# A two-layer encoder: the first MLP's down projection as seven products, and the conditioning in other pieces and on another engine

## The chip, the cores and the metric

The kernel runs on one core of a Trainium2 chip. A core has TensorE (PE in the profile; its weight loads are PEld) for matrix products, VectorE (DVE), ScalarE (ACT) and GpSimd (POOL) for elementwise work, and SyncE (SP), which here issues nearly all DMA transfers. The metric is the device time of one execution in microseconds (us), as the median of several runs.

## The reference

One inference step of two layers over 1024 prompt tokens and 32 sample tokens, of width 1024, with an MLP of hidden width 4096. The prompt and the sample each have one conditioning vector c. For layer l:

```python
u   = x * (1 + sc1) + sh1                       # sh, sc, g: six parts of silu(c) @ w_ada[l] + b_ada[l]
y   = mlstm(u)                 (layer 0)  or  band_attention(u)  (layer 1)
x   = layer_norm(ALPHA * x + (1 + g1) * y, ln_g[l, 0], ln_b[l, 0])
u   = x * (1 + sc2) + sh2
f   = jnp.square(jax.nn.relu(u @ w_up[l])) @ w_down[l]
x   = layer_norm(ALPHA * x + (1 + g2) * f, ln_g[l, 1], ln_b[l, 1])
```

Layer 0 mixes with an mLSTM (four heads, causal convolution, gated matrix memory in chunks), layer 1 with attention over a band of chunks and a shared key and value projection, which has a conditioning of its own (`w_ada_kv`). The outputs are the two final x, and the caches and states of the mixers. All is fp32.

## The kernel before

**Tokens and precision.** All T = 1056 tokens lie in the free dimension, the features on the 128 partitions, 8 rows deep. There are two ways to cut the tokens: blocks `TBS` of 384, 384 and 288, and quarters of `QN` = 264. An fp32 product is done in three matmuls: each operand is split into a high part (rounded by ScalarE) and the rest (subtracted by VectorE, `split`), and `proj` (L110 to L120) adds high by high (L118), high by low (L119) and low by high (L120) into one PSUM bank. There are eight banks.

**Layout in SBUF.** `U` holds the modulated input u, high and low, for all tokens; `uap` is a view of it. `acc` holds x, and takes the gated outputs; in the first layer it is three tiles, one for each block. A ring has three `raw` rooms (weights as they are loaded) and six `wc` rooms (their split forms). `wblock` loads 512 rows by 256 columns of a weight into a raw room and splits it. `tmp_t` gives one of five small rooms.

**Order.** The program is written as a stream of matmul groups. Beside it `Flow` keeps a list of side tasks, written as generators; every group of matmuls calls `flow.tick(columns / 96)`, and a task that has yielded a number goes on when so many ticks have passed; `flow.finish` runs a task to its end at once. A quarter's tile of an up projection is 2.75 ticks. The order of each engine's instructions follows this text, except where a region gives PE's order by hand (the seven products, L1314 on). A DMA on SP's queue waits there for the room it fills, and the DMAs behind it wait too.

**Stages.** PE runs through: the first projections; the mLSTM; its output projection (`out_proj`, L988), whose last step for a block starts a side task `norm` that also writes u for the MLP into U; the first MLP (`mlp`, L1006); q, keys and values; the attention; its output projection; the second MLP (`mlp7`, L1118); the last norm, which goes out by rows.

**The first MLP, `mlp`.** The hidden width goes in eight groups of 512. For each group there are four up tiles by three token blocks (`up`, L1016), kept in five `h` rooms as high and low of the squared relu, and eight down tiles by three blocks (`down`, L1031), each of which VectorE adds into acc with the gate (`add_gated_at`). Up of the next group is interleaved with down of this one. In the last group the ups are ordered so that the first block's down, and with it the norm that q needs, comes before the last ups (L1075 to L1080).

**The second MLP, `mlp7`.** Up goes first and whole: 16 pieces of 256 hidden features, by quarters (`up_tile`, L1166). Two hidden halves by two token halves make a 2x2 block, and down is a 2x2 by 2x2 block product in Winograd's form with seven products in place of eight. ScalarE and VectorE make seven operand forms of each piece (tiles `H`, three rooms, and `HL`, one room), and SP stores them to DRAM (`hd`, 1848 KB a piece and token half). The first 14 of the 16 pieces go this way, in four groups `GRP` of 3, 4, 3 and 4; the last two are done plainly: up in `up_plain` (L1180), stored to `hpl`, and down in the usual three matmuls at the end. Before the products, `forms` (L1221) makes the seven weight forms of a pair of output tiles from four blocks of w_down, and `Rooms` (L1103) hands out SBUF rooms into which `fill` loads operands `fx` by SP; some rooms are free at once (`f4`), others are what held u, free when the up has read it (`L.rooms`). `prep(i)` starts the loads of unit i's weights, the following steps of its generator do the sums and the splits. Up goes on `up_weights` loaded during the attention's output projection (`early_up`), so that PE finds weights there. `L1` holds what differs by layer.

**The conditioning.** `ada_cols` (L225) computes silu(c) @ w_ada without PE: for each 256 columns, the 1024 weight rows come in two loads of 512; VectorE multiplies each of the 8 rows of 128 by a scalar per partition and adds up (`aacc`, L238 and L241), once for the prompt and once for the sample, then transposes and reduces; PE sums what is left over partitions in four small matmuls per 1024 columns. Layer 0's part runs as a side task in the mLSTM (`ada_l0`, in one room of the ring, `ada_room`); the first 2048 columns of it come earlier. All of layer 1's and the key/value part (`ada_rest`, L1382) runs as a side task of the first MLP, from the third block's first up on, with waits `ADA_B` of 4, 2 and 1 ticks. It ends with `combine`, which folds a norm's gain and the conditioning together, and with `bias_table` for the attention; the first MLP's last norm waits for it (L1400).

## Time and profile before

| | |
|---|---|
| median of three runs | 2478.76 us (2478.34 to 2480.81) |
| profiled execution, its own time | 2479.81 us |
| its span | 2478.0 us, at a mean granted clock of 0.992 |
| PE, share of the span | 97% |
| DVE, ACT, POOL | 71%, 41%, 7% |
| DMA | 318.10 MB, 128 GB/s over the span |

A line of the groups reads: line of the kernel, engine, operation, output <- inputs by the program's names, partitions x elements, count, then busy time of the group and mean ns of one, then the idle time of the engine just before them with what ended most of it. A line that starts with a time is one instruction (or a run of equal ones): start, duration in us, engine, line, operation. For PE the durations of single matmuls overlap, so the steps between starts tell its pace. "granted clock" is TensorE's clock as the throttle let it run, as a share of full speed.

### The profile page before, as it was taken

The page shows a single profiled execution, that of the slowest core. Times are in us where ns is not written, and L with a number is a line of the kernel's source. Part 1 is how long each engine was busy: PE and PEld are TensorE (multiplying, and loading weights), DVE is VectorE, ACT ScalarE, POOL GpSimd, SP SyncE. Part 2 cuts the span into 40 slices and gives each one's busy share as a digit, 9 for nine tenths or more (in the row PEclk, how much of TensorE's full clock was granted, in tenths as well). Part 3 has the DMA queues.
Part 4 walks back from the last instruction along what each step waited for, and adds up shares of the span by engine and source line. Part 5 has one row for each costly group of instructions (what it writes and reads, how often), then busy time and mean ns, then how long its engine had stood idle before and what let it go on. Part 6 is the DMA issues. An engine that isn't in the chain of part 4 may idle for free.

```text
span 2478.0 us, 42688 instructions
## 1 busy us (share of the span) xinstructions
PE 2413.7 (97%) x16844; PEld 2315.4 (93%) x16844; DVE 1759.7 (71%) x4038; ACT 1016.9 (41%) x2118; POOL 168.6 (7%) x315
## 2 busy tenths in 40 slices
PE   7999999999999999999999999999999999999997
PEld 4999999999999999999999867789999999899997
DVE  4899999788679679677597667746853442776758
ACT  4644456382211212212266556654754443221212
POOL 0211100000000000000001134410000000000003
PEclk9999999999999999999999989999999999999999
DMA  8433224313224224234122310050375646767632
GB/s 297 122 110 101 84 88 129 107 35 119 77 87 137 84 86 135 80 92 142 43 98 82 91 40 1 18 147 27 134 251 212 215 179 254 262 239 273 255 130 72
DMA packets 236220, 318.10 MB, mean 128 GB/s; under 512 B 11624, under 2 KB 185084, under 8 KB 234996
## 3 DMA queue, kind: packets, MB, share of 16 engines
q1 hardware_dynamic: 236020, 315.38, 38.8%
q8 instruction: 132, 2.16, 0.4%
q14 instruction: 68, 0.56, 0.1%
HBM read 242.79 MB, written 74.91 MB: 128 GB/s over the span
## 4 chain that ended last, share of the span: by engine, by line
PE 78%; DVE 8%; DMA 6%; ACT 2%; issue 1%; POOL 0%; SPq 0%; DVEq 0%; POOLq 0%; ACTq 0%
PE up L118 10%; PE up L120 10%; PE up L119 9%; PE dn L1283 9%; PE dn L119 5%; PE dn L118 5%; PE dn L120 5%; DMA fx<-hd 3%; PE pv L1608 2%; PE pt L1588 2%; PE s L1558 2%; PE o L118 1%; PE o L119 1%; PE o L120 1%; PE op_b L118 1%
## 5 line engine op out<-in xcount | busy, mean ns | idle before, releaser
L120 PE MATMUL up<-u,w_up 128*128 128x264 f32 x1024 | 292.9, 286 | 0.0
L118 PE MATMUL up<-u,w_up 128*128 128x264 f32 x1024 | 292.4, 286 | 0.0
L119 PE MATMUL up<-u,w_up 128*128 128x264 f32 x1024 | 291.1, 284 | 0.0
L1283 PE MATMUL dn<-fx,wf 128*128 128x264 f32 x2208 | 275.3, 286 | 7.9 <-DMA fx<-hd 7.4
L1283 PEld LDWEIGHTS dn<-fx,wf 128*128 128x128 f32 x2208 | 272.2, 189 | 9.7 <-issue 4.6
L119 PE MATMUL dn<-h,w_dn 128*128 128x384 f32 (+1 forms) x768 | 249.5, 325 | 0.0
L118 PE MATMUL up<-U,w_up 128*128 128x384 f32 (+1 forms) x768 | 249.2, 324 | 0.0
L119 PE MATMUL up<-U,w_up 128*128 128x384 f32 (+1 forms) x768 | 247.9, 323 | 0.0
L118 PE MATMUL dn<-h,w_dn 128*128 128x384 f32 (+1 forms) x768 | 247.8, 323 | 0.0
L120 PE MATMUL up<-U,w_up 128*128 128x384 f32 (+1 forms) x768 | 247.6, 322 | 0.0
L120 PE MATMUL dn<-h,w_dn 128*128 128x384 f32 (+1 forms) x768 | 247.3, 322 | 0.0
L119 PEld LDWEIGHTS up<-u,w_up 128*128 128x128 f32 x1024 | 193.9, 189 | 0.0
L118 PEld LDWEIGHTS up<-u,w_up 128*128 128x128 f32 x1024 | 193.8, 189 | 0.0
L120 PEld LDWEIGHTS up<-u,w_up 128*128 128x128 f32 x1024 | 193.3, 189 | 0.0
L986 DVE SCALAR_TENSOR_TENSOR ACC<-dn,ada,ACC 128x264 f32<-128x264 f32 (+4 forms) x328 | 131.7, 426 | 86.4 <-PE dn L1283 74.6
L238 DVE SCALAR_TENSOR_TENSOR aacc<-rada,cs,aacc 128x256 f32<-128x256 f32 x448 | 190.3, 477 | 0.0
L986 DVE SCALAR_TENSOR_TENSOR acc<-dn,ada,acc 128x384 f32<-128x384 f32 (+2 forms) x256 | 119.4, 486 | 47.4 <-PE dn L120 46.3
L1025 ACT ACTIVATE r<-up 128x384 f32<-128x384 f32 (+1 forms) x96 | 44.3, 463 | 246.9 <-PE up L120 238.4
L119 PEld LDWEIGHTS dn<-h,w_dn 128*128 128x128 f32 x768 | 144.4, 188 | 0.2 <-DVE h L1028 0.2
L120 PEld LDWEIGHTS dn<-h,w_dn 128*128 128x128 f32 x768 | 144.5, 188 | 0.0
L120 PEld LDWEIGHTS up<-U,w_up 128*128 128x128 f32 x768 | 144.3, 188 | 0.0
L118 PEld LDWEIGHTS up<-U,w_up 128*128 128x128 f32 x768 | 144.2, 188 | 0.1
(354 smaller groups left out, 5957.4 us busy)
## 6 DMA issues: line engine op xcount, KB each, us to landing
hd<-HL SPq DMA_DIRECT2D x28, 1848.0 KB
raw_up<-in_w_up_dram SPq DMA_DIRECT2D x68, 512.0 KB
rada<-in_w_ada_dram SPq DMA_DIRECT2D x64, 512.0 KB
fx<-hd SPq DMA_DIRECT2D x37, 528.0 KB
raw_dn<-in_w_down_dram SPq DMA_DIRECT2D x36, 512.0 KB
ada_room<-in_w_ada_dram SPq DMA_DIRECT2D x32, 512.0 KB
fx<-hd SPq DMA_DIRECT2D x50, 264.0 KB
fx<-hd SPq DMA_DIRECT2D x16, 792.0 KB
```

The source lines that it names most:

```text
L118: nc.tensor.matmul(ps, wh, mov(0, k), start=(k == 0), stop=False)
L119: nc.tensor.matmul(ps, wh, mov(1, k), start=False, stop=False)
L120: nc.tensor.matmul(ps, wl, mov(0, k), start=False, stop=(k == nk - 1))
L238: nc.vector.scalar_tensor_tensor(acc[:, cnd], raw[:, k], sc, acc[:, cnd], op0=ALU.mult, op1=ALU.add)
L986: nc.vector.scalar_tensor_tensor(xs, ps[:, off + o:off + o + mm_], gate[:, fc, cnd:cnd + 1], xs, op0=ALU.mult, op1=ALU.add)
L1025: nc.scalar.activation(r, ps[:, :n], AF.Relu)
L1283: nc.tensor.matmul(p, ws[w][:, wl, k], t[:, s0, xl], start=first and k + n_ == 0, stop=k == kg - 1 and n_ == 2, skip_group_check=not first)
L1558: nc.tensor.matmul(s[:, b, :w], qst, kk[i][:, g, k0 + j0:k0 + j0 + w], start=(i == 0), stop=(i == 1))
L1588: nc.tensor.transpose(pt[:kp, j - j0, pr * P:(pr + 1) * P], ps_[pr][:, j * P:j * P + kp], ident)
L1608: nc.tensor.matmul(pv[64 * e:64 * e + 64, :nq], V[:kp, vt0 + j, g * 64:(g + 1) * 64], pts[e][:kp, j, :nq], start=(j == 0), stop=(j == nt - 1))
```

## The change

The first MLP also goes through `mlp7`, by a new class `L0`. `mlp` and the three-tile acc are removed; acc is one tile `ACC0`, cut into block views. Rooms for operands are U's two halves by columns, once the up has read them, so a load of rows goes to rows that lie apart. The up weights of the first pieces are loaded in the mLSTM's output projection (`early_up0`, and `up_weights(0, 0)` after the second block's end). The plain pieces' down at the end goes by the blocks `TBS`, and each block's end starts that block's norm as before. In q, ACC0's room is given up once all three norms have ended, which is asked for at the second block.

In `mlp7`, for both layers: the first unit's weight loads (`prep(0)`) are issued before the operand loads, the second unit's (`prep(1)`) before the last piece's first half; later ones (`prep(i + 2)`) one product later than before. In `forms` two of four sums are written in place. The plain pieces' results go through two rooms `hl` throughout, not partly through the ring.

The conditioning: in `ada_cols` (now used for layer 0 alone) the sample's products and sums go to GpSimd, as a multiplication into a side buffer and an addition. A new `ada_more` does the same in pieces of 512 (or 256) columns and loads of two rows of 128, each one ahead. What `ada_rest` did is cut in three: `ada_up` in the first MLP's up (columns 0 to 3071 of layer 1, the key/value part, and columns 3072 to 4095), `ada_down` in its products (4096 to 5119, in 256 columns), `ada_last` in the second MLP's up (5120 to 6143, the last gate).

```diff
                     for cnd in range(2):
                         sc = cs[:, 4 * half + k, cnd:cnd + 1]
-                        if half or k:
+                        if cnd:
+                            pr = tmp_f([P, 256], f"apr_{base}_{j}_{half}_{k}") if half or k else acc[:, 1]
+                            nc.gpsimd.tensor_scalar(pr, raw[:, k], sc, 0.0, op0=ALU.mult, op1=ALU.add)
+                            if half or k:
+                                nc.gpsimd.tensor_add(acc[:, 1], acc[:, 1], pr)
+                        elif half or k:
...
+    def ada_more(parts, nb, mk, tmp_f, raw_f, step):
+        n = nb * P
+        todo = [(src, c0, base, j, k0) for src, c0, base, nch in parts for j in range(0, nch, nb) for k0 in range(0, KC, 2)]
+        def load(i):
+            if i == len(todo):
+                return None
+            src, c0, base, j, k0 = todo[i]
+            raw = raw_f([P, 2, n], f"rada_{base}_{j}_{k0}")
+            nc.sync.dma_start(raw, src[k0 * P:(k0 + 2) * P, c0 + j * P:c0 + (j + nb) * P].rearrange(
+                "(k p) c -> p k c", p=P))
+            return raw
+        raw = load(0)
+        for i, (_, _, base, j, k0) in enumerate(todo):
+            ahead = load(i + 1)
+            yield step[0][i % len(step[0])]
+            if k0 == 0 and nb == 4:
+                accs_ = [tmp_f([P, n], f"aacc{cnd}_{base}_{j}") for cnd in range(2)]
+            elif k0 == 0:
+                acc3 = tmp_f([P, 3, n], f"aacc_{base}_{j}")
+                accs_ = [acc3[:, cnd] for cnd in range(2)]
+            for k in range(2):
+                for cnd in range(2):
+                    sc = cs[:, k0 + k, cnd:cnd + 1]
+                    if cnd:
+                        pr = accs_[1] if k0 + k == 0 else tmp_f([P, n], f"apr_{base}_{j}_{k0}_{k}") if nb == 4 else acc3[:, 2]
+                        nc.gpsimd.tensor_scalar(pr, raw[:, k], sc, 0.0, op0=ALU.mult, op1=ALU.add)
+                        if k0 + k:
+                            nc.gpsimd.tensor_add(accs_[1], accs_[1], pr)
+                    elif k0 + k:
+                        nc.vector.scalar_tensor_tensor(accs_[cnd], raw[:, k], sc, accs_[cnd], op0=ALU.mult, op1=ALU.add)
+                    else:
+                        nc.vector.tensor_scalar(accs_[cnd], raw[:, k], sc, None, op0=ALU.mult)
+            raw = ahead
+            if k0 < KC - 2:
+                continue
+            cxf = cx.rearrange("p g b -> p (g b)")
+            for cnd in range(2):
+                at = tmp_f([P, n], f"aat{cnd}_{base}_{j}")
+                nc.vector.transpose(at, accs_[cnd])
+                o0 = j % 8 * 8 + 4 * nb * cnd
+                nc.vector.tensor_reduce(out=cxf[:, o0:o0 + 4 * nb], in_=at.rearrange("p (b i) -> p b i", i=32),
+                                        axis=mybir.AxisListType.X, op=ALU.add)
+            if (j + nb) % 8 == 0:
+                yield step[1]
...
-    ADA_B = (4.0, 2.0, 1.0)
+    ADA_U, ADA_D, ADA_1 = ((5.5, 5.5, 2.75), 8.0), ((11.0,), 20.0), ((11.0,), 20.0)
     NOW = True
     TAIL = (1.0, 1.5)
-    W00 = (6.0, 12.0, 0.0, 0.0, 0.0, 3.0)
+    W00 = ((6.0, 12.0, 0.0, 0.0, 0.0, 3.0), (6.0, 12.0, 0.0, 0.0, 0.0, 3.0), (16.0, 14.0, 0.0, 0.0, 0.0, 3.0))
...
-        def mlp(hp, l, gate, order, before_tb, after_tb, last):
-            w_up, w_dn = a["w_up"][l], a["w_down"][l]
...
-            for i, ti in enumerate(order):
-                if i == 2:
-                    for t in order[:EARLY]:
-                        up(1, 0, t)
-                        early.add(t)
-                before_tb(ti)
...
-                        for c, ti in ((1, 0), (1, 1), (1, 2), (2, 0), (3, 0), (2, 1)):
-                            up(g, c, ti)
-                        finish(last[0])
-                        for c, ti in ((3, 1), (2, 2), (3, 2)):
-                            up(g, c, ti)
-                        rest = last[1:]
...
-    NW = 14
+    LP = NPB - 2
...
-                name = f"hl{l}_{pb}_{f}_{tp}"
-                hl = hlp.tile([P, 2, 2, QN], F32R, tag="hl", name=name, bufs=2) if pb == NPB - 1 else \
-                    ring.tile([P, 2, 2, QN], F32R, tag="raw", name=name, bufs=3)
+                hl = hlp.tile([P, 2, 2, QN], F32R, tag="hl", name=f"hl{l}_{pb}_{f}_{tp}", bufs=2)
                 split(hl[:, 0], hl[:, 1], r)
-                nc.sync.dma_start(hpl[2 * (pb - NW) + f, :, :, 2 * tp * QN:2 * (tp + 1) * QN],
+                nc.sync.dma_start(hpl[2 * (pb - LP) + f, :, :, 2 * tp * QN:2 * (tp + 1) * QN],
...
-            s1, s2, s3, s4 = (tmp_t([P, kg, P], f"s{i}_{nm}") for i in range(4))
+            s1, s2 = (tmp_t([P, kg, P], f"s{i}_{nm}") for i in range(2))
             nc.vector.tensor_add(s1, a21, a22)
             nc.vector.tensor_sub(s2, s1, a11)
-            nc.vector.tensor_sub(s3, a11, a21)
-            nc.vector.tensor_sub(s4, a12, s2)
-            for x, y in ((s2, s1), (s3, s4)):
+            nc.vector.tensor_sub(a11, a11, a21)
+            nc.vector.tensor_sub(a12, a12, s2)
+            for x, y in ((s2, s1), (a11, a12)):
...
+        prep(0)
         for t in f4:
             rooms.add(t)
         want += [(tp, f) for tp in L.pairs for f in order_f]
         fill(0, fx)
         for tp in L.pairs:
-            up_plain(NW, tp)
-        prep(0)
-        up_plain(NW + 1, tp0)
+            up_plain(LP, tp)
         for _ in range(4):
             got[0] = next(preps[0])
         prep(1)
+        up_plain(LP + 1, tp0)
         for t in L.rooms(tp0):
             rooms.add(t)
         fill(0, fx)
-        up_plain(NW + 1, tp1)
+        up_plain(LP + 1, tp1)
...
         rooms.add(f5_cm.__enter__().tile([P, KG, 2, QN], F32R, name=f"fx_5_{l}"))
         fill(0, fx)
+        L.down()
         with tc.manual_schedule(engines={mybir.EngineType.PE}):
...
-                    if j == 3:
+                    if j == 4:
                         prep(i + 2)
...
-    acc_cm, acc = open_acc(0, fwd)
-    mm, norm, _, out_proj, mlp, _, _ = make_layer(acc, bank, uap)
+    acc_cm0 = tc.tile_pool(name="acc0", bufs=1, side="right", reuse_waits="tile")
+    ACC0 = acc_cm0.__enter__().tile([P, KC, T], F32, name="ACC0")
+    acc = {ti: ACC0[:, :, t0:t0 + n] for ti, (t0, n) in enumerate(TBS)}
+    acc["all"] = ACC0
+    for ti in fwd:
+        t0, n = TBS[ti]
+        nc.sync.dma_start(acc[ti], xsp[0][:, :, t0:t0 + n])
+    mm, norm, _, out_proj, _, add_gated_at = make_layer(acc, bank, uap)
...
     def end_out0(ti):
-        norms[ti] = flow.add(norm(ti, 0, f"n00_{ti}", W00), now=NOW)
+        norms[ti] = flow.add(norm(ti, 0, f"n00_{ti}", W00[ti]), now=NOW)
+        if ti == 1:
+            wup0[0] = up_weights(0, 0)
...
-    out_proj([(0, 1, 2, 3)], fwd, oa_block, lambda hl, k, ti: uap(hl, k, *TBS[ti]), ada_part(0, 2), end_out0, "a")
-    def ada_rest():
-        yield from ada_cols(a["w_ada"][1], 0, 48, 48, mm, tmp_t, ADA_B)
-        yield from ada_cols(a["w_ada_kv"], 0, 96, 16, mm, tmp_t, ADA_B)
-        ada_fix(48, [(1, "sc"), (2, "g"), (4, "sc"), (5, "g")])
+    wup0 = {}
+    def early_up0(ti, pr):
+        if ti == 2 and pr < 2:
+            wup0[pr + 1] = up_weights(0, pr + 1)
+    out_proj([(0, 1, 2, 3)], fwd, oa_block, lambda hl, k, ti: uap(hl, k, *TBS[ti]), ada_part(0, 2), end_out0, "a",
+             after_pr=early_up0)
+    h_cm.__exit__(None, None, None)
+    def ada_up():
+        yield from ada_more([(a["w_ada"][1], 0, 48, 24), (a["w_ada_kv"], 0, 96, 16), (a["w_ada"][1], 3 * D, 72, 8)],
+                            4, mm, tmp_t, raw_tile, ADA_U)
+        ada_fix(48, [(1, "sc"), (2, "g")])
         ada_fix(96, [(1, "sc")])
         combine(1, lng(1), lnb(1), ada_part(1, 1), ada_part(1, 0))
-        combine(2, lng(2), lnb(2), ada_part(1, 4), ada_part(1, 3))
         yield
         bias_table()
+    def ada_down():
+        yield from ada_more([(a["w_ada"][1], 4 * D, 80, 8)], 2, mm, tmp_t, tmp_t, ADA_D)
+        ada_fix(48, [(4, "sc")])
+        combine(2, lng(2), lnb(2), ada_part(1, 4), ada_part(1, 3))
+    def ada_last():
+        yield from ada_more([(a["w_ada"][1], 5 * D, 88, 8)], 4, mm, tmp_t, raw_tile, ADA_1)
+        ada_fix(48, [(5, "g")])
     def before0(ti):
         flow.finish(norms[ti])
         if ti == 2:
-            norms["ada"] = flow.add(ada_rest())
+            norms["ada"] = flow.add(ada_up())
...
-    mlp(hp, 0, ada_part(0, 5), fwd, before0, end0, TBS)
-    h_cm.__exit__(None, None, None)
+    U4 = U[:, :2 * UF].rearrange("p (l k t) -> p l k t", l=2, k=KC)
+    class L0:
+        l, alloc, add, gate, wups = 0, mm, add_gated_at, ada_part(0, 5), wup0
+        pairs, quarters, blocks = (0, 1), (0, 1, 2, 3), TBS
+        ready, after = before0, end0
+        def u(hl, k, q):
+            return uap(hl, k, q * QN, QN)
+        def down():
+            flow.finish(norms["ada"])
+            norms["ada"] = flow.add(ada_down())
+        def rooms(pr):
+            return [U4[:, hl, KG * i:KG * (i + 1), 2 * pr * QN:2 * (pr + 1) * QN].rearrange("p k (l t) -> p k l t", l=2)
+                    for hl in range(2) for i in range(2)]
+        def end(f4p):
+            pass
+    mlp7(L0)
...
-                acc_cm[ti].__exit__(None, None, None)
+                if ti == 1:
+                    flow.finish(norms[2])
+                    acc_cm0.__exit__(None, None, None)
...
         def ready(i):
             flow.finish(norms[rev[i]])
+            if i == 2:
+                norms["ada"] = flow.add(ada_last())
+        def down():
+            flow.finish(norms["ada"])
```

93 lines of the change are left out of this document (16 added, 77 removed).

## The prediction

> **What bounds the kernel now.** I read the page's sums, then the stages one by one, then the pace of single matmuls, and then each other engine where it ends a wait of PE. One program runs on one core, so the core's span is the time.
>
> ```profile
> span 2478.0 us, 42688 instructions
> PE 2413.7 (97%) x16844; PEld 2315.4 (93%) x16844; DVE 1759.7 (71%) x4038; ACT 1016.9 (41%) x2118; POOL 168.6 (7%) x315
> ```
>
> The profiled execution took 2479.81 us, 1.8 us more than its span, and 1.05 us more than the median of 2478.76. PE is busy almost throughout; whether it is also at its pace is seen in the stages (columns: window, length, busy time of PE, PEld, DVE, ACT, POOL, granted clock, DMA share, GB/s).
>
> ```profile
> 95.00:440.00 345.00, 341.49 (x2251) 323.99 (x2252) 318.27 (x925) 182.38 (x484) 38.89 (x107) 1.00 0.34 105
> 575.00:1158.00 583.00, 582.91 (x3660) 580.99 (x3659) 448.80 (x990) 122.30 (x197) 0.00 (x0) 1.00 0.33 102
> 1900.00:2000.00 100.00, 100.00 (x822) 100.00 (x821) 43.85 (x55) 46.18 (x70) 0.00 (x0) 1.00 0.59 206
> 2110.00:2409.00 299.00, 291.11 (x2358) 289.25 (x2357) 207.93 (x460) 63.27 (x114) 0.00 (x0) 0.99 0.63 229
> ```
>
> In the first MLP (second row) PE never waits, at full clock: only fewer or shorter matmuls can shorten it. The fourth row is the second MLP's down, which already runs as seven products; there PE idles 8 of 299 us. The stage boundaries of both MLPs, and the steps between matmuls of 384 and of 264 columns:
>
> ```profile
> 515.10 0.34 PE L118 MATMUL up<-U,w_up 128*128 128x384 f32 x1
> ...
> 599.96 0.33 PE L120 MATMUL dn<-h,w_dn 128*128 128x384 f32 x1
> ...
> 601.01 0.33 PE L120 MATMUL dn<-h,w_dn 128*128 128x384 f32 x1
> 601.18 0.29 PE L118 MATMUL dn<-h,w_dn 128*128 128x288 f32 x1
> ...
> 1222.20 0.33 PE L118 MATMUL up<-U,w_up 128*128 128x384 f32 x1
> ...
> 1263.51 0.29 PE L120 MATMUL dn<-h,w_dn 128*128 128x288 f32 x1
> 1263.64 0.34 PE L118 MATMUL q<-U,w_q 128*128 128x384 f32 x1
> ...
> 1732.22 0.28 PE L118 MATMUL up<-u,w_up 128*128 128x264 f32 x1
> ...
> 1839.57 0.29 PE L118 MATMUL up<-u,w_up 128*128 128x264 f32 x1
> ...
> 1844.20 0.29 PE L120 MATMUL up<-u,w_up 128*128 128x264 f32 x1
> ...
> 2110.23 0.40 PE L1283 MATMUL dn<-fx,wf 128*128 128x264 f32 x2
> ...
> 2408.81 0.30 PE L118 MATMUL dn<-hs,w_dn 128*128 128x288 f32 x1
> ```
>
> Six steps of 384 columns take 1.05 us (0.175 each), 38 of 264 take 4.63 us (0.122 each), and 288 takes 0.13 (1263.51 to 1263.64). A pass over all 1056 columns is 2 x 0.175 + 0.13 = 0.48 us in blocks and 4 x 0.122 = 0.49 in quarters: the narrower pieces cost nothing worth counting.
>
> **The change part by part.** First the seven products. The counts come from the groups (the last number before the bar):
>
> ```profile
> L119 PE MATMUL dn<-h,w_dn 128*128 128x384 f32 (+1 forms) x768 | 249.5, 325 | 0.0
> L1283 PE MATMUL dn<-fx,wf 128*128 128x264 f32 x2208 | 275.3, 286 | 7.9 <-DMA fx<-hd 7.4 <-issue 0.3
> L1283 PE MATMUL dn<-fx_w,wf 128*128 128x264 f32 x144 | 19.5, 284 | 0.0
> ```
>
> Now the first MLP's down is 3 x 768 matmuls, 768 passes of 0.48, so 369 us, and its up the same. In the new form it is 2208 + 144 = 2352 products of 0.122 (287 us) for 14 of the 16 pieces of the hidden width, and an eighth of 369 (46 us) for the last two: 333, or 36 us less. That is the gain if PE keeps pace. What such a stage costs in practice the second MLP shows, since its matmuls are the same ones: up 1732.22 to 2110.23 is 378.0 us, products to 2408.81 are 298.6, and with 46 for the plain rest that makes 722.6. The first MLP now takes 515.10 to 1263.64, 748.5. **Term one: -26 us**, with the second MLP's own losses in it. Of these, the waits at the start of the products are the largest:
>
> ```profile
> PE dn L1283 <- DMA fx<-hd: 7.4, 6, 3.1
> 2125.50:2132.50 7.00, 4.71 (x20) 4.47 (x21) 1.09 (x3) 0.51 (x1) 0.00 (x0) 0.51 1.03 404
> 2084.24 6.59 SPq L1117 DMA_DIRECT2D fx<-hd  x7
> 2091.06 0.52 SPq L1191 DMA_DIRECT2D hpl<-hl  x1
> 2092.92 1.04 SPq L1228 DMA_DIRECT2D rdn<-in_w_down_dram  x2
> 2103.71 4.49 SPq L1228 DMA_DIRECT2D rdn<-in_w_down_dram  x2
> 2108.26 4.20 SPq L1117 DMA_DIRECT2D fx<-hd  x8
> SPq L1228 <- DVE s L1247: 10.3, 2, 6.7
> ```
>
> PE waits 7.4 us for operands, and the clock granted after it is halved for 7 us, which loses another 3.4: 10.8 us in all. The first raw weights (L1228) go out 8.7 us after the first operands, the second pair holds SP's queue at 2103.71 until VectorE has used the first, and the operands behind it leave only at 2108.26. **Weights ahead of operands** takes that hold away, but the DMA share there is 1.03, so the bytes themselves still bound it: between 0 and -10.8, I take -4, the hold of 4.49 us, once in each MLP: -8. The two buffers that now carry all eight stores of the plain pieces can delay ScalarE by a store each; eight PSUM banks (8 x 24 x 0.122 = 23 us of PE) cover that: 0 to +3, I take +1. Half of the first MLP's operands go to rows of U that lie apart, in shorter pieces than now: 0 to +3, I take +1.
>
> **The conditioning** leaves VectorE in part. Removed are 512 instructions of 256 columns on the first line below; added are 512-column pieces, one sample's half of them as two instructions on GpSimd:
>
> ```profile
> L238 DVE SCALAR_TENSOR_TENSOR aacc<-rada,cs,aacc 128x256 f32<-128x256 f32 x448 | 190.3, 477 | 0.0
> L555 DVE SCALAR_TENSOR_TENSOR y<-qkp,pt,y 128x1059 f32<-128x1059 f32 x24 | 31.9, 1330 | 0.0
> L1574 POOL TENSOR_SCALAR p<-p,mx 128x512 f32<-128x512 f32 x8 | 5.6, 695 | 5.8 <-DVE mx L1573 5.7
> 2463.27 1.28 POOL L971 TENSOR_TENSOR yb<-yb,gb 128x512 f32<-128x512 f32 x1 [2.33 <-DVE yb L970]
> 1344.12 2.91 DVE L1488 TENSOR_TENSOR x<-x,kvss 128x1024 f32<-128x1024 f32 x1 [0.53 <-POOL x L1487]
> 1347.65 1.23 DVE L1488 TENSOR_TENSOR x<-x,kvss 128x1024 f32<-128x1024 f32 x1
> ACT HL L89 <- DMA hd<-HL: 13.2, 8, 3.2
> ```
>
> On the line through 477 at 256 columns and 1330 at 1059 a piece of 512 costs VectorE 0.75 us; GpSimd pays 0.70 for the product and 1.28 for the sum. Two pieces are 8 steps, 13 tiles of ticks plus 3 of the longer wait: 16 tiles of 24 x 0.122, 47 us of PE. In that time GpSimd works 16 x 0.70 + 14 x 1.28 = 29 us, VectorE 16 x 0.75 = 12 beside its 43.85% (21 us) of the third stage row. Each alone fits. But they disturb each other: L1488 takes 1.23 us alone and 2.91 when it starts while GpSimd sums (1344.12). If every instruction of the one shut out the other, 29 + 12 + 21 = 62 us would be needed in 47, 15 us more in each of six rounds: 90, of which the 23 us of PSUM banks hide a part. Bounds: 0 to +67. Under the same stage ScalarE already waits 13.2 us for the one HL buffer's store, and the conditioning adds half a megabyte per step to a queue at 0.59; a late store there also opens the operand room late. The low end is nearer, because waits overlap the issue of the waiting instruction and VectorE is not in two-operand work all the time: I take **+8**. If the cover of 23 us were used up, each us of lag would be one of PE.
>
> The Trainium skill, "SBUF — State Buffer", section "Who interferes with whom", says that a VectorE instruction with two SBUF inputs contends with a GpSimd instruction that reads SBUF, and that the loser blocks for the whole instruction. The row at 1344.12 agrees: 1.68 us lost. By that rule the upper bound above is the one to take; it is rival one.
>
> **In the mLSTM** half of the conditioning's 256 VectorE instructions move to GpSimd. They free some 128 x 0.478 = 61 us of VectorE's 318, and GpSimd gets as many pairs beside its 39 us. PE's waits in that stage bound the gain:
>
> ```profile
> L238 DVE SCALAR_TENSOR_TENSOR ada_room<-ada_room,cs 128x256 f32<-128x256 f32 x224 | 99.4, 478 | 3.3 <-DMA ada_room<-in_w_ada_dram 3.2
> PE cu L634 <- DVE hn L660: 1.6, 2, 1.0
> PE cu L634 <- DVE sm L649: 0.7, 2, 0.5
> ```
>
> With PE idle 3.5 of 345 us there, -3.5 to +6 (the slower sums ahead of qc on GpSimd and of the last weights on SP's queue); I take 0.
>
> **The end.** The first block's norm begins when its last down is added. That is now at 1222.20, with 41 us of matmuls until q needs it. Afterwards only the plain blocks two and three follow: 96 x (0.175 + 0.13) = 29 us. Norm one is written out in 27 us of ticks, and its last writes now come just at q:
>
> ```profile
> 1263.43 0.70 ACT L330 ACTIVATE ut_n<-acc,comb 128x384 f32<-128x384 f32 x1
> ```
>
> 0 to +8, I take +3. The third norm is now finished before the second block's q, whose outputs wait for the accumulator's room; with 25 us of q for block one ahead and eight banks, PE does not see it. The part of the conditioning that goes to the second MLP's up (VectorE 44%) and to the first's down is small and spread: 0. The up's start, where the second MLP waits for a norm, has two whole blocks of cover in the first: 0.
>
> **Sum**: -26 - 8 + 1 + 1 + 8 + 0 + 3 = -21 from 2479.8, so 2459; the median lies 1 lower, so **2458 us**, faster by 0.8%.
>
> **The rivals.**
>
> One, **the two engines shut each other out** (slower). Place: the first MLP's up, while the conditioning runs. For it: 1344.12. Against: in that row both were long instructions at once, and GpSimd is idle there 18 of 47 us. Price: of the 90 us of collisions, less the 23 us of banks, half would leave 22 in place of my 8 (-7 in all, still faster at 2472), three quarters 45 (+16: 2495), all of them 67 (+38: 2517). The sign turns once the lag past the banks exceeds 29 us. I put it at 2495.
>
> Two, **the transition eats it**: late stores of HL open the room late, the operands arrive late by as much and the clock halves. For it: 10.8 us lost now at DMA share 1.03. Price: +15 in the first MLP and no gain from the weights in either (+8): 2481, no change.
>
> Three, **the waits vanish**: both transitions lose nothing (-22 instead of -8) and the lag stays in the buffers (-8): 2436.
>
> That the change doesn't do what it says would show as 768 matmuls per line of the old form; the code leaves no room for it.
>
> **How the numbers follow.** Forecast 0.55, rival one 0.25, two 0.12, three 0.08. The forecast's own range is 2444 to 2472, its terms' bounds without rival one's; the range that holds 8 of 10 reaches down near rival three and up to rival one: 2440 to 2500. Some 0.2%, or 5 us, is what a measurement can tell from no change. Faster: the forecast, three, and a low case of two, 0.64; same: most of two and a little of one, 0.10; slower: 0.26.
>
> **What would show it.** Right: 2352 products of 0.122 us in the first MLP's down, its stages at 378 and about 295 us, PE without idle in up while GpSimd is at some 60%; 4 us less wait at the start of the second MLP's products. Rival one would show as VectorE near 100% and stretched durations of its 512-column pieces, with PE waiting for w_up or for PSUM; two as waits for fx and a halved clock near the first products; the end as a wait of q for U. The forecast is wrong if the first MLP's up takes over 400 us.

## The result, and the profile after

The changed kernel takes 2627.91 us (median of four runs, 2623.5 to 2630.63) against 2478.55 us before: 1.0599 times as long, 95% interval 1.0583 to 1.0615. The forecast was 2458 us, and its range ended at 2500. The profiled execution took 2630.63 us, the head of its page:

```profile
span 2628.8 us, 45796 instructions
PE 2437.5 (93%) x17948; PEld 2327.8 (89%) x17948; DVE 1862.6 (71%) x3722; ACT 1090.0 (41%) x2242; POOL 714.9 (27%) x825
```

PE's share falls from 97% to 93%, and GpSimd's rises from 7% to 27%. Where the 151 us of span went is read from the first matmuls of the stages, first in the kernel before, then in the changed one (start, duration of one, line, operation):

```profile
71.70 0.42 PE L118 MATMUL qk<-U,w_qk 128*128 128x384 f32 x1
...
417.69 0.44 PE L118 MATMUL op_a<-U,w_oa 128*128 128x384 f32 x1
```

```profile
72.41 0.42 PE L118 MATMUL qk<-U,w_qk 128*128 128x384 f32 x1
...
488.80 0.44 PE L118 MATMUL op_a<-U,w_oa 128*128 128x384 f32 x1
...
600.53 0.28 PE L118 MATMUL up<-U,w_up 128*128 128x264 f32 x1
...
1041.75 0.77 PE L1252 MATMUL dn<-fx,wf 128*128 128x264 f32 x5
...
1357.29 0.34 PE L118 MATMUL dn<-hs,w_dn 128*128 128x384 f32 x1
...
1404.80 0.34 PE L118 MATMUL q<-U,w_q 128*128 128x384 f32 x1
```

Differences of such starts give the stages of all kernels in this study (us; "mLSTM" is from the first qk to the first op_a, the first MLP is up + products + plain down, the last column the median of the runs):

| kernel | mLSTM | its output projection | first MLP: up + products + plain | q to attention | second MLP: up, products | median |
|---|---|---|---|---|---|---|
| before | 346.0 | 97.4 | 748.5 | 368.4 | 378.0, 298.6 | 2478.55 |
| changed | 416.4 | 111.7 | 441.2 + 315.5 + 47.5 = 804.3 | 368.3 | 378.3, 307.3 | 2627.91 |
| mLSTM undone (e1) | 347.2 | 97.6 | 441.4 + 315.2 + 47.5 = 804.1 | 369.5 | 377.6, 304.6 | 2544.47 |
| MLP pieces undone (e2) | 417.7 | 112.4 | 391.1 + 318.2 + 47.5 = 756.7 | 368.4 | 377.7, 304.2 | 2579.71 |
| both undone (e3) | 346.8 | 95.5 | 393.2 + 314.6 + 47.5 = 755.3 | 368.4 | 377.6, 304.9 | 2494.02 |
| and old order (e6) | 345.8 | 97.5 | 390.4 + 314.7 + 47.5 = 752.6 | 369.1 | 377.6, 300.6 | 2489.65 |
| and no conditioning in the first MLP (e8) | 347.9 | 97.0 | 375.3 + 311.0 + 47.8 = 734.2 | 372.3 | 377.7, 298.3 | 2469.33 |

So of 151 us, 85 are in the mLSTM and the projection behind it (70.4 and 14.3), 56 in the first MLP, 9 in the second one's products. A stage's "up" runs to the first product, so it holds PE's wait for the first operands, if there is one. Windows in the changed kernel (columns as in the prediction):

```profile
95.00:440.00 345.00, 293.20 (x1820) 272.00 (x1821) 265.34 (x722) 143.97 (x400) 173.92 (x288) 0.92 0.26 79
...
800.00:900.00 100.00, 89.84 (x697) 88.33 (x696) 97.58 (x94) 39.89 (x60) 84.84 (x54) 0.91 0.81 270
900.00:1000.00 100.00, 84.47 (x652) 83.32 (x650) 72.98 (x80) 34.02 (x55) 57.28 (x41) 0.90 0.68 228
1000.00:1100.00 100.00, 81.25 (x587) 78.63 (x586) 53.27 (x107) 27.71 (x55) 18.35 (x19) 0.88 0.81 287
```

In the mLSTM's window, where PE was busy 341 of 345 us before, it is now busy 293 at a clock of 0.92. The window catches less of the stage's work than before (1820 matmuls against 2251), so VectorE's lower time in it (265 against 318) is no relief. Over the whole stage VectorE's busy time falls only from 319.5 to 306.9 us, where 61 were to be freed. PE's idle time there grows from 5.7 to 54.2 us, and its busy time, for the same matmuls, from 340.3 to 362.2 at a clock of 0.93: 48 of the 70 us are waits, 22 go with the lower clock. In the first MLP's up (800 to 900) VectorE is at 98% with GpSimd at 85%. VectorE near 100% is one of the signs that the prediction gave for its rival one.

### The profile page after: what moved, and what is told of

Same layout as the page of the kernel before. It is cut to its first block, busy times and chain, and to the rows that moved or that the text cites. A ratio compares the mean times of both kernels' runs of the same rounds, so it can differ in the third digit from the quotient of the medians.

```text
span 2628.8 us, 45796 instructions
## 1 busy us (share of the span) xinstructions
PE 2437.5 (93%) x17948; PEld 2327.8 (89%) x17948; DVE 1862.6 (71%) x3722; ACT 1090.0 (41%) x2242; POOL 714.9 (27%) x825
## 4 chain that ended last, share of the span: by engine, by line
PE 60%; DVE 14%; DMA 12%; POOL 8%; ACT 3%; issue 3%; SPq 0%; POOLq 0%; DVEq 0%; ACTq 0%
PE dn L1252 18%; PE up L120 6%; PE up L118 6%; PE up L119 6%; DMA ada_room<-in_w_ada_dram 3%; DMA fx<-hd 3%; POOL ada_room L240 2%; POOL ada_room L242 2%; PE pv L1627 2%; PE pt L1607 2%; PE s L1577 2%; DVE aacc L299 2%; DMA hd<-HL 1%; DMA rada<-in_w_ada_dram 1%; POOL aacc L297 1%
## 5 line engine op out<-in xcount | busy, mean ns | idle before, releaser
L1252 PE MATMUL dn<-fx,wf 128*128 128x264 f32 x3108 | 407.8, 288 | 22.5 <-DMA fx<-hd 16.7
L1252 PEld LDWEIGHTS dn<-fx,wf 128*128 128x128 f32 x3108 | 394.1, 191 | 25.7 <-issue 11.7
L1036 DVE SCALAR_TENSOR_TENSOR ACC<-dn,ada,ACC 128x264 f32<-128x264 f32 (+5 forms) x648 | 263.4, 430 | 185.2 <-PE dn L1252 161.2
L118 PE MATMUL up<-U,w_up 128*128 128x264 f32 x1024 | 300.4, 293 | 25.2 <-ACT w_up L89 19.5
L120 PE MATMUL up<-U,w_up 128*128 128x264 f32 x1024 | 298.4, 292 | 18.8 <-DVE w_up L90 18.8
L119 PE MATMUL up<-U,w_up 128*128 128x264 f32 x1024 | 298.0, 291 | 0.0
L118 PEld LDWEIGHTS up<-U,w_up 128*128 128x128 f32 x1024 | 200.3, 196 | 26.7 <-ACT w_up L89 20.6
L89 ACT CAST wf<-rdn 128x384 fp32r<-128x384 f32 (+1 forms) x160 | 84.7, 566 | 334.7 <-PE dn L1252 153.6
L120 PEld LDWEIGHTS up<-U,w_up 128*128 128x128 f32 x1024 | 199.6, 195 | 21.4 <-DVE w_up L90 21.0
L90 DVE TENSOR_TENSOR HL<-H,HL 128x264 fp32r<-128x264 f32 x112 | 142.1, 1269 | 101.0 <-ACT HL L89 100.7
L119 PEld LDWEIGHTS up<-U,w_up 128*128 128x128 f32 x1024 | 200.3, 196 | 0.0
L89 ACT CAST HL<-H 128x264 fp32r<-128x264 f32 x112 | 102.8, 962 | 222.0 <-DMA hd<-HL 202.6
L1252 PE MATMUL dn<-U,wf 128*128 128x264 f32 x1308 | 181.4, 291 | 6.6 <-DMA U<-hd 6.1
L1252 PEld LDWEIGHTS dn<-U,wf 128*128 128x128 f32 x1308 | 170.8, 193 | 9.2 <-issue 5.9
```

The costliest lines, as they stand in the source:

```text
L89: nc.scalar.copy(dst_h, src)
L90: (eng or nc.vector).tensor_sub(dst_l, src, dst_h.bitcast(F32))
L118: nc.tensor.matmul(ps, wh, mov(0, k), start=(k == 0), stop=False)
L119: nc.tensor.matmul(ps, wh, mov(1, k), start=False, stop=False)
L120: nc.tensor.matmul(ps, wl, mov(0, k), start=False, stop=(k == nk - 1))
L1036: nc.vector.scalar_tensor_tensor(xs, ps[:, off + o:off + o + mm_], gate[:, fc, cnd:cnd + 1], xs, op0=ALU.mult, op1=ALU.add)
```

## The experiments

**One part undone at a time.** The sample's half goes back to VectorE, in the mLSTM (e1) or in the pieces of the MLPs (e2, the same edit in `ada_more`); e3 does both.

```diff
-                        if cnd:
-                            pr = tmp_f([P, 256], f"apr_{base}_{j}_{half}_{k}") if half or k else acc[:, 1]
-                            nc.gpsimd.tensor_scalar(pr, raw[:, k], sc, 0.0, op0=ALU.mult, op1=ALU.add)
-                            if half or k:
-                                nc.gpsimd.tensor_add(acc[:, 1], acc[:, 1], pr)
-                        elif half or k:
+                        if half or k:
```

> The changed kernel with one part undone: in the mLSTM the sample's half of the conditioning is back on VectorE. From the first qk matmul to the first of the output projection the changed kernel takes 416 us, the kernel before 346. Theory (GpSimd's half is what stretches the mLSTM): 346 us again, and the wait of 9 us at the output projection's first weights goes too, 2545 to 2560 us in all. Rival (the stretch has another cause, such as the order of loads): still over 400 us there, 2610 to 2630 in all.

> The changed kernel with another part undone: layer 1's conditioning keeps its wide pieces, its loads and its place, but the sample's half is VectorE's too; the mLSTM is as in the changed kernel. Theory (GpSimd and VectorE shut each other out in the first MLP's up): up falls from 441 us to 380 to 395, although VectorE gets 72 us more to do by its own durations, 2567 to 2585 us in all. Rival one (bytes: the loads of the conditioning delay the stores of HL, and with them ScalarE): up stays at 430 or more, 2615 to 2630. Rival two (VectorE is simply full): up at 400 to 430.

> The changed kernel with the sample's conditioning on VectorE everywhere, in the mLSTM and in the pieces of the MLPs. If the two losses (the mLSTM's 84 us, the first up's 50) are independent, they add: 2628 - 84 - 49 = 2490 to 2500 us, so still slower than the kernel before, because the first MLP's up then takes 391 and its products 318 us where the prediction had 378 and 298.6. If one loss hid part of the other: 2505 to 2520, or below 2485.

All three came as the theory had them, e1 half a us below its range: 2544.47, 2579.71 and 2494.02 us. Undone alone the parts give 83.4 and 48.2 us, together 133.9, so they are nearly independent. What is left, e3, is still slower than the kernel before (1.0061, interval 1.0046 to 1.0076).

How the first MLP's up was lost shows in VectorE's groups over that stage, first in the changed kernel, then in e2, where the same kind of instruction runs without GpSimd beside it (count, then busy time and mean ns):

```profile
L299 DVE SCALAR_TENSOR_TENSOR aacc<-rada,cs,aacc 128x512 f32<-128x512 f32 x84 | 109.1, 1298 | 1.9
L90 DVE TENSOR_TENSOR w_up<-raw_up,w_up 128x1024 fp32r<-128x1024 f32 x30 | 44.2, 1484 | 0.2 <-ACT w_up L89 0.2
L1135 DVE TENSOR_TENSOR H<-H 128x528 f32<-128x528 f32 x28 | 26.7, 952 | 2.2 <-ACT H L1133 2.0
L308 DVE STREAM_TRANSPOSE aat<-aacc 128x512 f32<-128x512 f32 x24 | 16.5, 699 | 10.6 <-POOL aacc L297 10.0
```

```profile
L294 DVE SCALAR_TENSOR_TENSOR aacc<-rada,cs,aacc 128x512 f32<-128x512 f32 x168 | 117.5, 746 | 6.2 <-DMA rada<-in_w_ada_kv_dram 5.5 <-DMA rada<-in_w_ada_dram 0.7
L90 DVE TENSOR_TENSOR w_up<-raw_up,w_up 128x1024 fp32r<-128x1024 f32 x30 | 36.1, 1220 | 1.9 <-ACT w_up L89 1.8
L1130 DVE TENSOR_TENSOR H<-H 128x528 f32<-128x528 f32 x28 | 19.6, 701 | 4.8 <-ACT H L1128 4.8
L303 DVE STREAM_TRANSPOSE aat<-aacc 128x512 f32<-128x512 f32 x24 | 15.9, 692 | 0.0
```

The accumulation takes 1298 ns instead of 746, so half the instructions (84 of 168) cost VectorE nearly the same time (109.1 against 117.5 us): the offload freed almost nothing. Instructions with two inputs in SBUF that had nothing to do with the conditioning stretch too (952 against 701, 1484 against 1220). Of those with one input, the transpose does not (699, 692); the multiplication that begins each sum does (820 against 477). The Trainium skill, "SBUF — State Buffer", section "Who interferes with whom", has this as its rule: two SBUF inputs on VectorE against a GpSimd instruction that reads SBUF, one of them blocked for the whole of the other. The rows above agree on the two-input instructions; a group's mean does not show whether one is blocked for the whole of the other.

A slower VectorE is felt where a chain is tight, here at the one HL room. The starts of ScalarE's first and last copy into HL, of 28, in the changed kernel's first MLP and in the second MLP of the kernel before:

```profile
626.87 0.41 ACT L89 CAST HL<-H 128x264 fp32r<-128x264 f32 x1
...
999.22 1.81 ACT L89 CAST HL<-H 128x264 fp32r<-128x264 f32 x2
```

```profile
1761.22 0.41 ACT L89 CAST HL<-H 128x264 fp32r<-128x264 f32 x1
...
2076.24 1.81 ACT L89 CAST HL<-H 128x264 fp32r<-128x264 f32 x2
```

27 steps take 372 us, 13.8 each, where they took 315, 11.7 each; and 11.7 is what PE needs to make their input (4 x 24 x 0.122). A step is ScalarE's copy, VectorE's subtraction and the store, one behind the other. From the copy's start to the subtraction's end it takes 6.1 us on average (4.2 in e2, 3.9 in the second MLP before), from the store to the next copy 7.6 (7.9 and 7.8). So all that is added lies in VectorE's part, and there is no slack to take it up. The chain of HL now sets the pace, ScalarE stands in it, and the splits of the up weights behind it on ScalarE come late. The waits of this stage in the changed kernel (total, times, longest):

```profile
ACT HL L89 <- DMA hd<-HL: 112.4, 20, 16.3
...
PE up L118 <- ACT w_up L89: 19.5, 5, 9.3
PE up L120 <- DVE w_up L90: 18.8, 8, 3.9
```

PE waits 38 of the 63 us for weights; the rest lies in smaller waits and in the granted clock, which goes down to 0.88 to 0.91 after them (windows above).

**The mLSTM: slowed instructions, or waits?** Two ends: e5 leaves the sample's half out on every engine (GpSimd's three lines go, and VectorE sets `acc[:, 1]` to zero once for each 256 columns), e4 keeps GpSimd busy on data of its own (`side` is a new buffer of 256 columns, `csf` the constants `cs`) and sets the sample's half to zero in the same way.

```diff
-                            nc.gpsimd.tensor_scalar(pr, raw[:, k], sc, 0.0, op0=ALU.mult, op1=ALU.add)
-                            if half or k:
-                                nc.gpsimd.tensor_add(acc[:, 1], acc[:, 1], pr)
+                            csf = cs.rearrange("p k c -> p (k c)")
+                            nc.gpsimd.tensor_scalar(side, csf, sc, 0.0, op0=ALU.mult, op1=ALU.add)
+                            if half or k:
+                                nc.gpsimd.tensor_add(side, side, csf)
+                            else:
+                                nc.vector.memset(acc[:, 1], 0.0)
...
+    side = A.tile([P, 256], F32, tag="side", name="side")
```

> The changed kernel with the sample's half of the mLSTM's conditioning left out on every engine (set to zero, so the output differs): VectorE has 128 instructions less than in the kernel before and GpSimd none of them. This prices what could have been won there. By the waits of PE before (3.5 us of 345) the stage comes to 342 to 347 us, 2545 to 2558 in all; if VectorE's load was a hidden limit there, below 340.

> The changed kernel, but in the mLSTM GpSimd's products and sums work on a buffer of their own and constant data, with the same number, kind and width, so that neither the load room nor VectorE waits for them (the sample's conditioning is left out and set to zero, so the output differs). Theory one (slowed instructions: both engines shut each other out at SBUF): the stage stays near 400 us, 2605 to 2630 in all. Theory two (waits: the one load room and the sum are late because of GpSimd, and VectorE stands in order behind them): the stage falls to 350 to 370, 2560 to 2580 in all.

e5 took 2545.4 us, the stage 349.8, just above its range: with the work gone altogether nothing is won over e1 (2544.47). There was never a gain to be had here. e4 took 2641.23 us, but for a reason that neither theory had. The waits of that stage:

```profile
PE ae_ps L589 <- ACT stk L582: 62.7, 1, 62.7
DVE stk L566 <- POOL stk L547: 58.3, 1, 58.3
```

Waiting for nothing, GpSimd's instructions were put in one heap at the front of its queue, and a memset that the gates need (`stk`) stood behind 103 of the 128 pairs, where in the changed kernel it stands before all of them. So an engine's order is not that of the program's text alone, as it was put above. This run decides nothing between the two. In e4b a token, a copy of one column on VectorE, ties each pair to VectorE's step (against e4):

```diff
+                            tok = tmp_f([j // 2 * 8 + half * 4 + k], "tok")
+                            nc.vector.tensor_copy(tok, acc[:, 0, 0:1])
-                            nc.gpsimd.tensor_scalar(side, csf, sc, 0.0, op0=ALU.mult, op1=ALU.add)
+                            nc.gpsimd.tensor_scalar(side, csf, tok, 0.0, op0=ALU.mult, op1=ALU.add)
```

> As the decoupled run (GpSimd's products and sums in the mLSTM on a buffer and data of their own, the sample left out), but each pair starts only when VectorE has done its own instruction of that step, so that GpSimd works at the same moments as in the changed kernel while nobody waits for it. Theory one (slowed instructions at SBUF): the stage from the first qk to the output projection, 416 us in the changed kernel and 346 before, stays at 395 or more. Theory two (VectorE and the one load room wait for a late GpSimd): 345 to 365, 2550 to 2575 us in all.

The mLSTM took 364.0 us, the end that theory two gave, but the total of 2588.76 lies above it, since the output projection took 120.9. In the mLSTM, then, 52 of the 69 us by which the changed kernel (416.4) exceeds e1 (347.2) go when nobody waits for GpSimd. The 17 that stay hold the slowed instructions, and the tokens, which cost VectorE 16.0 us themselves. The 23 us that the output projection takes beyond e1's are another matter, as the waits there show:

```profile
POOL side L242 <- DVE ada_room L241: 35.9, 4, 31.6
PE adas L262 <- DVE cx L256: 17.3, 1, 17.3
```

PE stands 17.3 us for the last sums of the conditioning. GpSimd holds nothing up here: it is itself idle for 31.6 us, up to 441.40. The last three loads of the conditioning leave SP's queue only from 445.65 on, behind loads of the output weights. No run shows what such a late place costs by itself.

In e4b GpSimd is as slow as in the changed kernel (857 and 725 ns there); VectorE's accumulation is stretched by about half as much (531 ns, against 594 there and 475 in e5), so some of the 52 us may be the milder stretch and not the waits:

```profile
L248 DVE SCALAR_TENSOR_TENSOR ada_room<-ada_room,cs 128x256 f32<-128x256 f32 x98 | 52.0, 531 | 5.1 <-DMA ada_room<-in_w_ada_dram 3.9
...
L244 POOL TENSOR_TENSOR side<-side,cs 128x256 f32<-128x256 f32 x98 | 82.8, 845 | 7.6
L242 POOL TENSOR_SCALAR side<-cs,ada_room 128x256 f32<-128x256 f32 x112 | 82.5, 737 | 68.8 <-DVE ada_room L241 44.1 <-DVE sm L720 11.4 <-DVE sm L717 5.8
```

In the changed kernel VectorE stands idle twice for them (idle time and what ended it, last column), and its instructions in time show one case:

```profile
L244 DVE SCALAR_TENSOR_TENSOR ada_room<-ada_room,cs 128x256 f32<-128x256 f32 x91 | 54.0, 594 | 20.8 <-DMA ada_room<-in_w_ada_dram 20.2
...
L251 DVE STREAM_TRANSPOSE ada_room<-ada_room 128x512 f32<-128x512 f32 x12 | 8.5, 710 | 21.7 <-POOL ada_room L242 17.5 <-POOL vt L507 4.2
```

```profile
228.05 1.62 DVE L619 SCALAR_TENSOR_TENSOR y<-qkp,pt,y 128x1059 f32<-128x1059 f32 x1
228.51 1.75 POOL L242 TENSOR_TENSOR ada_room<-ada_room 128x256 f32<-128x256 f32 x1
...
233.89 0.48 POOL L240 TENSOR_SCALAR ada_room<-ada_room,cs 128x256 f32<-128x256 f32 x1
234.40 0.37 SPq L232 DMA_DIRECT2D ada_room<-in_w_ada_dram  x1
237.92 0.48 DVE L244 SCALAR_TENSOR_TENSOR ada_room<-ada_room,cs 128x256 f32<-128x256 f32 x1 [3.48 <-DMA ada_room<-in_w_ada_dram]
238.32 0.16 DVE L713 RECIPROCAL sm<-sm 128x1 f32<-128x1 f32 x1
```

GpSimd, stretched by VectorE's wide convolution steps (the sum at 228.51 takes 1.75 us, where the group's mean is 0.86), reads the load room last at 233.89; only then can the next load go (234.40), and VectorE holds its whole queue 3.48 us for it, the chunk's own reciprocal at 238.32 included. PE waits for that chain, in the mLSTM more than for anything else:

```profile
PE cu L698 <- DVE hn L724: 29.0, 12, 5.7
```

**The part alone, in the kernel before.** Both the mLSTM's and the old first MLP's conditioning give the sample's half to GpSimd; but for the side buffer's width in the load room all else is as before.

```diff
-                        if half or k:
+                        if cnd:
+                            pr = tmp_f([P, 256], f"apr_{base}_{j}_{half}_{k}") if half or k else acc[:, 1]
+                            nc.gpsimd.tensor_scalar(pr, raw[:, k], sc, 0.0, op0=ALU.mult, op1=ALU.add)
+                            if half or k:
+                                nc.gpsimd.tensor_add(acc[:, 1], acc[:, 1], pr)
+                        elif half or k:
```

> The kernel before, with one part of the change alone: the sample's products and sums on GpSimd, in the mLSTM and in the old first MLP, which keeps its form, its 256-column pieces and its places. Theory for the mLSTM (the loss is this part's own): first qk to output projection 410 to 425 us instead of 346, and 10 to 15 more in the output projection. Theory for the old first MLP (a slowed VectorE costs nothing where it had 134 of 583 us idle and no chain as tight as the one HL room): 748 to 755 us instead of 748.5. Rival (the two engines shut each other out enough to hold PE there too): 770 or more. Total 2555 to 2575 us by theory, 2585 or more by the rival.

2568.76 us, 1.0372 (1.0354 to 1.0389), as the theory had it: the mLSTM took 417.9 us and its projection 113.0, and the old first MLP 749.5 against 748.5. There the accumulation was slowed too, by the groups of that stage:

```profile
L243 DVE SCALAR_TENSOR_TENSOR aacc<-rada,cs,aacc 128x256 f32<-128x256 f32 x224 | 151.5, 676 | 4.1
```

676 ns where VectorE alone needs 477, and PE lost 1 us: a disturbance of this kind cost nothing there. That this is so because no chain is tight is argued; GpSimd's work was also spread thinner (busy 167 of the 300 us from 700 on, against 85 of 100 above).

**The seven products by themselves.** All three have the conditioning on VectorE, as e3. e6 puts back the old order at the start of the products, e8 takes the conditioning out of the first MLP as well, e9 leaves only its loads.

```diff
-        prep(0)
         for t in f4:
             rooms.add(t)
...
         for tp in L.pairs:
             up_plain(LP, tp)
+        prep(0)
+        up_plain(LP + 1, tp0)
         for _ in range(4):
             got[0] = next(preps[0])
         prep(1)
-        up_plain(LP + 1, tp0)
...
-                    if j == 4:
+                    if j == 3:
                         prep(i + 2)
```

> The run with all conditioning on VectorE, and in addition the order of the kernel before at the start of the products: operand loads before the first unit's weights, the last piece's first half before their sums, and the later weights one product earlier. Theory (the new order puts the split of the plain piece behind sums and additions that wait for products, so the last store, and the operand loads behind it on SP's queue, go out late): the first MLP's products fall from 318 us to 300 to 308 and the second's from 304 to 298 to 300, 2470 to 2483 us in all. Rival (the waits there come from the rows of U lying apart or from the bytes alone): the first's stay at 315 or more, the total falls by 5 us at most.

```diff
-        yield from ada_more([(a["w_ada"][1], 0, 48, 24), (a["w_ada_kv"], 0, 96, 16), (a["w_ada"][1], 3 * D, 72, 8)],
-                            4, mm, tmp_t, raw_tile, ADA_U)
+        nc.vector.memset(ada[:, 48:112], 0.0)
...
-        yield from ada_more([(a["w_ada"][1], 4 * D, 80, 8)], 2, mm, tmp_t, tmp_t, ADA_D)
+        yield 20.0
```

> The run with the old order and all conditioning on VectorE, with layer 1's conditioning (products, sums and loads) left out of the first MLP, its up and its products, and set to zero (the output differs); the mLSTM's and the second MLP's part stay. This tests the prediction's first term by itself: that the first MLP in the new form costs what the second one does, 378 + 298.6 + 46 = 722.6 us. Theory (it does, and the 30 us missing are the conditioning's): up 377 to 381, products 298 to 304, 2450 to 2462 us in all. Rival (U's rooms or the blocks of the accumulator cost something of their own): the products stay above 308.

In e9 the loop over `k` and `cnd` in `ada_more`, with the transposes and reductions behind it, becomes one instruction of one column for each load:

```diff
+            nc.vector.tensor_scalar(accs_[0][:, k0 // 2:k0 // 2 + 1], raw[:, 1, n - 1:n], cs[:, 0, 0:1], None, op0=ALU.mult)
```

> The same kernel of the old order with the conditioning's loads kept in all MLP stages, each read by one instruction of one column, and its products and sums left out (the output differs). If VectorE's time is what the conditioning costs in the first MLP (12 us in up, 14 in the products): times of the run without conditioning within 4 us. If its bytes and its places in SP's queue cost it: times of the run with the old order, up 388 to 391 and products 310 to 315.

e6: 2489.65 us (1.0039, 1.0025 to 1.0054), 4 less than e3, at the edge of what the intervals tell apart. The second MLP's products fell from 304.9 to 300.6, the first's did not (314.6 to 314.7): the theory's forecast came, nearly, in the second MLP, and the rival's, nearly, in the first (315 or more, the total 5 us lower at most). PE's wait for operands in U's rooms fell there from 10.7 to 6.4 us, but 3.0 came back as a wait for weight forms. What the new order does is seen in e2, VectorE and SP's queue in time:

```profile
993.95 0.63 ACT L89 CAST hl<-hr 128x528 fp32r<-128x528 f32 x1
994.07 0.49 DVE L1031 SCALAR_TENSOR_TENSOR ACC<-dn,ada,ACC 128x264 f32<-128x264 f32 x1 [1.45 <-PE dn L1247]
...
998.45 0.49 DVE L1031 SCALAR_TENSOR_TENSOR ACC<-dn,ada,ACC 128x264 f32<-128x264 f32 x1 [0.60 <-PE dn L1247]
998.85 0.70 DVE L90 TENSOR_TENSOR hl<-hr,hl 128x528 fp32r<-128x528 f32 x1
...
999.58 0.52 SPq L1155 DMA_DIRECT2D hpl<-hl  x1
1000.20 4.66 SPq L1083 DMA_DIRECT2D U<-hd  x7
```

The plain piece's split (998.85) stands behind five additions that wait for products, its store holds SP's queue to 999.58, and the operand loads behind it come late.

e8 took 2469.33 us, above its range of 2450 to 2462, and only 9 us below the kernel before (0.9963, 0.9947 to 0.9979): without conditioning the first MLP takes 734.2, its up 375.3 and its products 311.0, so the rival's number holds for the products. PE waits 15.3 us in them (6.7 in the same kernel's second MLP), at a clock of 0.97 (0.99). The largest wait is for operands in U's rooms:

```profile
PE dn L1242 <- DMA U<-hd: 7.8, 3, 4.9
```

Why these come late, no run shows. e9 took 2483.05 us. PE's up ended 376 us after its start there too, so in up the 15 us by which e6 lies above e8 are VectorE's sums and not the loads; but then PE waited 16.7 us for the first operands, because loads into U, which wait until the up has read it, stood in SP's queue ahead of the last stores of HL that the operands follow:

```profile
877.43 2.74 SPq L1070 DMA_DIRECT2D U<-hd  x4
880.26 0.56 SPq L1123 DMA_DIRECT2D hd<-HL  x1
880.88 6.24 SPq L1070 DMA_DIRECT2D U<-hd  x4
895.42 0.36 SPq L1123 DMA_DIRECT2D hd<-HL  x1
...
897.64 6.45 SPq L1070 DMA_DIRECT2D fx<-hd  x7
```

SP's queue has another order in each version, so e9 doesn't say what the loads cost in the products.

**Other places for the conditioning.** Two attempts to make e6 faster than the kernel before, e7 by two more pieces in the products, e10 by two pieces in q; in both the steps of those that stay in up are spread evenly.

```diff
-        yield from ada_more([(a["w_ada"][1], 0, 48, 24), (a["w_ada_kv"], 0, 96, 16), (a["w_ada"][1], 3 * D, 72, 8)],
+        yield from ada_more([(a["w_ada"][1], 0, 48, 24), (a["w_ada_kv"], 0, 96, 16)],
...
-        yield from ada_more([(a["w_ada"][1], 4 * D, 80, 8)], 2, mm, tmp_t, tmp_t, ADA_D)
+        yield from ada_more([(a["w_ada"][1], 3 * D, 72, 8), (a["w_ada"][1], 4 * D, 80, 8)], 2, mm, tmp_t, tmp_t, ADA_D)
```

> The run with the old order and all conditioning on VectorE, with two of twelve pieces moved from the first MLP's up to its products (in 256 columns, a step each 6.5 ticks) and the rest spread evenly. Theory (VectorE is full in up: 166 us of its own and 178 of conditioning in 378): up falls from 391 to 380 to 385 us, products rise by at most 5, 2465 to 2480 us in all. Rival (the loads of the conditioning, not VectorE, cost the 13 us): up falls by no more than 3 us and the total is that of the run with the old order or above.

```diff
-        yield from ada_more([(a["w_ada"][1], 0, 48, 24), (a["w_ada_kv"], 0, 96, 16), (a["w_ada"][1], 3 * D, 72, 8)],
+        yield from ada_more([(a["w_ada"][1], 0, 48, 16), (a["w_ada_kv"], 0, 96, 16), (a["w_ada"][1], 3 * D, 72, 8)],
...
+    def ada_q():
+        yield from ada_more([(a["w_ada"][1], 2 * D, 64, 8)], 2, mm, tmp_t, tmp_t, ADA_Q)
+        ada_fix(48, [(2, "g")])
...
                 if ti == 1:
                     flow.finish(norms[2])
                     acc_cm0.__exit__(None, None, None)
+                    flow.add(ada_q())
```

> The run with the old order and all conditioning on VectorE, with the second gate's two pieces moved out of the first MLP's up to the q and key/value stages (in 256 columns) and the other ten spread evenly over up; two stay in the products. By the run with ten pieces in up (383 us) and the run with two in the products (315): the first MLP 745 us, the stages of q to attention 368 to 375, 2476 to 2484 us in all, no change against the kernel before. If q has no room for 30 us of VectorE: over 2490.

Both missed. e7: 2504.33 us; up fell to 383.3 as expected, but the products rose to 335.9, 21 us for two more pieces; PE waits 15.2 us there for VectorE's additions into ACC (4.6 in e6). e10: 2509.52 us; the first MLP took 754.3 and q to attention 391.6, 22 more. No version that does all the work beats the kernel before.

## Why the prediction was wrong, step by step

- **In the mLSTM: "0, from -3.5 to +6".** The step that failed first: 84.7 us with the output projection, half of the 170 by which the sum missed. The gain was bounded rightly by PE's waits (e5 shows none), the loss was not: only late work behind GpSimd's and SP's queues was priced, though the prediction itself told, one paragraph earlier, that the two engines shut each other out. What the runs showed: GpSimd's pair takes some 1.6 us where it takes 0.48 + 0.72 undisturbed (e4, from 100 to 113 us), the one load room and the transpose make VectorE wait for it in order (38 us idle in the rows above), and PE waits for the chain of a chunk on VectorE. With these waits gone, 52 of the mLSTM's 69 us go (e4b).
- **The conditioning in the first MLP: "+8, from 0 to +67".** The mechanism was rival one's, at its place, and its price nearly the upper bound: up took 441.2 instead of 378, 63 more, past the 400 at which the prediction called itself wrong; 50 of it goes with GpSimd (e2). The choice of the low end failed. It held that VectorE is not in two-operand work all the time and that GpSimd is idle 18 of 47 us; stretched, they are at 98% and 85% in the window at 800. That waits overlap the issue of the waiting instruction, its other reason, no run here puts a number on. And the 23 us of PSUM banks gave no cover, since PE stood waiting for weights and not for a bank, with ScalarE held in the HL chain.
- **The seven products: "-26".** Mis-sized: -14 without any conditioning (e8, 734.2 against 748.5), and +4 with it on VectorE (e6, 752.6). The second MLP's times were taken as the price of the form, but it had the stage to itself. Its up leaves VectorE 56% idle; in the old first MLP the conditioning was spread over 583 us, in which PE was busy 582.91.
- **Weights ahead: "-4 in each".** The sign failed: putting the old order back makes e3 4 us faster, and only the second MLP's products gain by it. The queue's hold that it was to remove was replaced by another, a split behind additions.
- **Buffers for the plain stores and U's rooms: "+1" each.** Not tried apart. At most they make the 12 us by which e8's products (311.0) exceed the second MLP's 298.6.
- **The end: "+3".** 47.5 us of plain down against 46, q to attention unchanged: about right.
- **The range and rivals.** Rival one was the right kind and was capped at 2517, since the same lock was not applied to the mLSTM; no case held both.

Open: how the mLSTM's 69 us divide exactly between waits and slowed instructions (e4b has tokens of its own and a milder stretch), what delays the conditioning's last loads there, and why the operands of the first MLP's products come late in U's rooms without any conditioning.

## What to carry to other kernels

Before work is moved from VectorE to GpSimd, count what each will run at the same time: in the first MLP's up, VectorE's instructions with two operands in SBUF stretched by 1.2 to 1.7 and GpSimd's beside them by 1.3 to 2.0, and the busy time that was to be freed came back as longer instructions. The price was then set by the nearest in-order wait: a shared load room, or a sum that VectorE reads back, turned GpSimd's lateness into VectorE's, and a chain with one buffer turned that into PE's. A stage's time measured without side work is no price for the same stage with it; ask first what the idle share it frees was used for.

## What the runs showed that was not expected

GpSimd's multiplication by a scalar, one input only, is stretched more than its sum of two: from 695 ns at 512 columns (before) to 1413 in the first MLP's up of the changed kernel, the sum from 1280 to 1625:

```profile
L297 POOL TENSOR_TENSOR aacc<-aacc,apr 128x512 f32<-128x512 f32 x84 | 136.5, 1625 | 3.4
L295 POOL TENSOR_SCALAR apr<-rada,cs 128x512 f32<-128x512 f32 x84 | 118.0, 1413 | 64.3 <-DMA rada<-in_w_ada_dram 61.8 <-DMA rada<-in_w_ada_kv_dram 1.9 <-DVE aat L308 0.2
```

And work that depends on nothing can be worse than work that waits: in e4 it cost PE 62.7 us in one stall, by its place in GpSimd's queue alone.
